# Fourteen block-product pairs instead of eleven, two rooms for their weights, and two u chunks moved behind the first v chunks

## The chip, the cores and the metric

The kernel runs on one core of a Trainium2 chip. The metric is the device time of one execution in microseconds, the median of several runs. Engines are named as the profile names them: PE (TensorE), DVE (VectorE), ACT (ScalarE), POOL (GpSimd), SP (SyncE, here only a queue of DMA issues).

## The reference, cut to what matters

One encoder layer on 256 tokens of width 1024: a modulated norm, a joint projection, two kinds of attention, an output projection, a second modulated norm, and then PEER, a retrieval of single-neuron experts, which takes most of the time. The reference gathers experts per token:

```python
ub = jnp.take(u_tab, ib, axis=0)            # 16384 experts x 1024
a  = jnp.einsum('td,ted->te', xb, ub)
w  = gb * jax.nn.gelu(a, approximate=False)
vb = jnp.take(v_tab, ib, axis=0)
y  = jnp.einsum('te,ted->td', w, vb)
```

Each token uses 8 x 16 experts with softmax gates. After it: x + gate2 * y, and a last norm.

## The kernel before, in words

The kernel gathers nothing. The 16384 experts are 128 chunks of 128. For each chunk i it computes a = u[i] times all 256 tokens (the first expert matmul), Gelu(a) times a gate table that is zero where a token does not use an expert, and adds weights times v[i] to y (the second expert matmul).

All weights are fp32 and are split in two fp32r parts: ACT copies `raw` to `hi` (L96), DVE or POOL computes `lo = raw - hi` (L97). A product is then three matmuls (`mm3`, L138 to L141): high by high, high by low, low by high. An `order` list names every unit of weights with a kind: "b" gives its L97 to POOL, "c" to DVE, and "s" marks a part of a pair, whose L97 is DVE's and which lies in the tile already. `unit()` hands out the units in that order and prepares one ahead (LEAD is 1). In the expert stages there are three buffers for `raw`, four for `hi`, three for `lo`: the `lo` of a unit can be written only when PE has done with the unit three before it, and a load can start only when the split of the unit three before has read its `raw`. All these loads are issued on SP, in order.

Stages, in order: projections, attention, the output projection, then the routing beside the first 36 u chunks (AHEAD), whose results lie in the tile GA, 256 columns to a chunk. Then the one-hot stage: for each of 64 groups of four tokens PE builds the gate table by one-hot matmuls (`gp`, L851), and between them runs u chunks 36 to 127 (`u_chunk`, 24 matmuls of 256 columns each into one of two PSUM buffers), followed by Gelu on ACT (L867) and the product with the gates on DVE (L868) into GB. A u chunk can start only when the PSUM buffer of the chunk two before it has been read by L868. BESIDE is the count of u chunks in this stage, HOLD how many of them are kept back until after the last group; BESIDE - HOLD is 89.

Then the second expert matmul, over a `plan` of steps. A plain step is one v chunk: weights of the experts (`gated`: ACT L883, DVE L884, three `wx` buffers), one unit of v, and 12 matmuls of 512 columns into the four PSUM accumulators `yp`. The last three chunks are done together at the end, so that the closing work on the first half of the tokens can begin early.

Some neighbouring chunks i and i+1 are done as a pair: a 2x2 by 2x2 block product by Strassen's scheme in Winograd's form, in seven products instead of eight. A product has three matmuls, so a pair has 21 matmuls instead of 24. For it DVE has to form four differences of v blocks (`pair_t13`, L917; `pair_t24`, L921 and L922), split them (`pair_split`, L925 on ACT, L926 on DVE), and form and split differences of the expert weights (`pair_s`, L934, L936, L937; `pair_a`, L943, L944). The pair's v chunks are loaded to a room inside GA (`bb`, the cells of chunks 12 to 19, whose values are used up by then) and the differences to `bt` (cells 20 to 27). Two parts of the room go through `unit()` as kind "s". `todo` places the steps of a pair a number of plan steps ahead of it: the load 6, `pair_s` 5, `pair_t13` 4, `pair_t24` 3, the splits 2 and 1.

SEVEN = (31, 8, 112) makes pairs of chunks 31, 39, ... 111: eleven, with six plain steps between two. The rows of `gate2` (another 8 DVE reductions, in GA cells 0 to 11) run at steps 12 to 28. After the last pair, `fold` takes one operation per plain step: it adds the pairs' accumulators and the residual up.

The order in which each engine gets its instructions is worked out when the kernel is built, from the program order, the dependencies and a list scheduler's estimate of times; DVE, ACT and SP then execute their lists strictly in that order.

Of the kernel before, what the change touches and what calls it, by code (L numbers as in the profile page):

```python
# [11 lines left out]
AF = mybir.ActivationFunctionType  # L12
# [4 lines left out]
S = 256  # L17
HD = 64
NH = 8
NKEY = 128  # L20
# [2 lines left out]
BIG = 1e30  # L23
LOW = -3e38
AHEAD = 36
BESIDE = 92
LEAD = 1
LATE = 5
E2AT = 0
HOLD = 3  # L30

SEVEN = (31, 8, 112)
ENDLEAD = 2
LAST = 3
FG0 = (("p", 0, 512), ("p", 512, 1024))
# [35 lines left out]
def body(tc, xT, cols, ada, w_in, e2, w_out, wq, sk, u, v, fg, const, dil, out):  # L71
    nc = tc.nc
    with ExitStack() as top:
# [29 lines left out]
        order = []  # L103
# [8 lines left out]
        order += [(wq[i], "b") for i in range(16)]  # L112
        order += [(u[i], "b") for i in range(AHEAD + BESIDE)]

        seven = [i for i in range(*SEVEN[:1], SEVEN[2]) if (i - SEVEN[0]) % SEVEN[1] == 0]
        plan = [i for i in range(NKEY - LAST) if i - 1 not in seven]
        parts = []
        for i in plan:
            order += [(p, "s") for p in range(2)] if i in seven else [(v[i], "c")]
        order += [(v[i], "c") for i in range(NKEY - LAST, NKEY)]  # L120
        ready = []
        loaded = []
# [3 lines left out]
        def unit():  # L126
            while len(ready) <= min(taken[0] + lead[0], len(order) - 1):
                i, kind = len(ready), order[len(ready)][1]
                if kind == "s":
                    ready.append(split(i, parts[order[i][0]], nc.vector))  # L130
                    continue
                taken[1] += kind == "a"
                eng = nc.gpsimd if kind == "b" or kind == "a" and taken[1] % 2 else nc.vector
                ready.append(split(i, loaded.pop(0) if loaded else load(i), eng))
            taken[0] += 1
            return ready[taken[0] - 1]

        def mm3(ps, wh, wl, ah, al, first, last):  # L138
            nc.tensor.matmul(ps, wh, ah, start=first, stop=False)  # L139
            nc.tensor.matmul(ps, wh, al, start=False, stop=False)  # L140
            return nc.tensor.matmul(ps, wl, ah, start=False, stop=last)  # L141

        def mmT(ps, hl, act):
            h = hl[0].rearrange("p (k c) -> p k c", k=8)
            l = hl[1].rearrange("p (k c) -> p k c", k=8)
            for k in range(8):
                ins = mm3(ps, h[:, k, :], l[:, k, :], act[0][:, k, :], act[1][:, k, :], k == 0, k == 7)
            return ins
# [13 lines left out]
        def act_tiles(name):  # L162
            return tuple(P0.tile([128, 8, S], F32R, tag="h" + x, name=name + x) for x in "hl")
# [19 lines left out]
        with ExitStack() as pre:  # L183
# [129 lines left out]
            for i in range(2):  # L313
                ps = PP.tile([128, 512], F32, tag="acc", name="silp")
# [314 lines left out]
            for i in range(NQ):  # L629
                hl = unit()  # L630
                ps = PM.tile([128, 512], F32, tag="mm", name="ps")
# [13 lines left out]
            for k in range(8):  # L645
                b = mod[:, 3, k:k + 1]
                if k % 2 == 0:
                    tt = PP.tile([128, 512], F32, tag=("PT", "acc")[k // 2 % 2], name="h2t")
                t, hi = tt[:, k % 2 * S:(k % 2 + 1) * S], h2[0][:, k, :]
# [7 lines left out]
            GA = GAP.tile([128, AHEAD, S], F32)  # L657
# [3 lines left out]
            def u_chunk(i):  # L661
                hl = unit()
                ps = PM.tile([128, 512], F32, tag="mm", name="ps")
                mm_ins[i] = mmT(ps[:, :S], hl, h2).ins
                return ps
# [149 lines left out]
        def cell(i, t0, t1):  # L815
            return GA[:, i, t0:t1] if i < AHEAD else GB[:, i - AHEAD, t0:t1]

        done = AHEAD
# [8 lines left out]
        def one_hots(n):  # L827

            if 4 * n >= S:
                return  # L830
            t0 = 4 * n
            jm = WK.tile([128, 4, 128], F32R, tag="wx", name="jm", bufs=WXB)
            gi = WK.tile([128, 4, 2, 128], F32R, tag="gi", name="gi", bufs=2)
            nc.vector.tensor_tensor(jm, iotaG[:, None, :].to_broadcast([128, 4, 128]),  # L834
                                    jT[:, t0:t0 + 4, None].to_broadcast([128, 4, 128]), op=OP.is_equal)
            for t in range(4):
                nc.vector.scalar_tensor_tensor(gi[:, t, :, :], iotaG[:, None, :].to_broadcast([128, 2, 128]),  # L837
                                               iT[:, t0 + t:t0 + t + 1],
                                               gT.bitcast(F32)[:, :, t0 + t, None].to_broadcast([128, 2, 128]),
                                               op0=OP.is_equal, op1=OP.mult)  # L840
            hot[n] = jm, gi
# [3 lines left out]
        for n in range(S // 4):  # L845
# [17 lines left out]
            one_hots(n + 2)  # L863
            while done - AHEAD < (BESIDE if t0 + 4 == S else (n + 1) * (BESIDE - HOLD) // (S // 4)):
                te = t0 + 4
                ps = u_chunk(done)
# [8 lines left out]
        with tc.tile_pool(name="py", bufs=1, space=bass.MemoryType.PSUM) as PY:  # L875
# [11 lines left out]
            def give(i, hl, T, f):  # L887
                ts, fs = slice(T * 128, (T + 1) * 128), slice(f * 512, (f + 1) * 512)
                wh, wl = W[i]
                mm3(yp[T][f], wh[:, ts], wl[:, ts], hl[0][:, fs], hl[1][:, fs], i == 0, i == NKEY - 1)  # L890

            def row(t):
                return bass.AP(tensor=t.tensor, offset=t.offset, ap=[[0, 128], [1, D]])
# [8 lines left out]


            bl = GA[:, 12:28, :].rearrange("p (b a) t -> p b (a t)", a=2)
            bb, bt = bl[:, 0:4, :], bl[:, 4:8, :]
            parts += [bb[:, 3:4, :], bb[:, 0:3:2, :]]
            sph, spl = (t.rearrange("p (b a) t -> p b (a t)", a=2) for t in act_tiles("sp"))
            P = {}
            AS = {}

            def pair_load(i):
                for e in range(2):
                    nc.sync.dma_start(bb[:, 2 * e:2 * e + 2, :], v[i + e].rearrange("p (f c) -> p f c", f=2))

            def pair_t13(i):

                nc.vector.tensor_tensor(bt[:, 0:2, :], bb[:, 1:4:2, :], bb[:, 0:2, :], op=OP.subtract)  # L917

            def pair_t24(i):

                nc.vector.tensor_tensor(bt[:, 2, :], bb[:, 3, :], bt[:, 0, :], op=OP.subtract)  # L921
                nc.vector.tensor_tensor(bt[:, 3, :], bb[:, 2, :], bt[:, 2, :], op=OP.subtract)  # L922

            def pair_split(n, m, src):
                nc.scalar.activation(sph[:, n:m, :], src, AF.Copy)  # L925
                nc.vector.tensor_tensor(spl[:, n:m, :], src, sph.bitcast(F32)[:, n:m, :], op=OP.subtract)  # L926
# [66 lines left out]


            p1, r, c12, c21 = (bt[:, n, :] for n in range(4))
            c22 = bb[:, 0, :]
            fold = [lambda: nc.scalar.activation(p1, P[1], AF.Copy)]
            fold += [lambda o=o, x=x, y=y: nc.vector.tensor_add(o, P[x], y) for o, x, y in ((r, 6, p1), (c12, 5, r), (c21, 7, r), (c22, 7, c12))]
            for n, c in enumerate((p1, c12, c21, c22)):
                t, fs = x1[n // 2], slice(n % 2 * 512, (n % 2 + 1) * 512)  # L1000
# [5 lines left out]
            todo = {}  # L1006
            for i in seven:
                at = plan.index(i)
                for d, f in ((6, pair_load), (5, pair_s), (4, pair_t13), (3, pair_t24),
                             (2, lambda i: pair_split(0, 2, bt[:, 0:2, :])), (1, lambda i: pair_split(2, 4, bt[:, 2:4, :]))  # L1010
                             ):
                    todo.setdefault(at - d, []).append((f, i))
            for n, i in enumerate(plan):
                nxt = plan[n + 1] if n + 1 < len(plan) else NKEY - LAST
                for f, p in todo.get(n, ()):
                    f(p)
                (pair_a if nxt in seven else gated)(nxt)
                if i in seven:
                    pair_products(i)
                    if i == seven[-1]:  # L1020
                        for dst, src in ((g2b, row(g2d)), (x1[0], x1d[0]), (x1[1], x1d[1]), (fgb, row(fg))):
                            nc.sync.dma_start(dst, src)
                        fold.pop(0)()
                    continue
                hl = unit()
                for T in range(2):
                    for f in range(2):
                        give(i, hl, T, f)
                if i >= 12 and i % 2 == 0 and (i - 12) // 2 < 9:
                    gate2((i - 12) // 2)  # L1030
                if i > seven[-1] and fold:
                    fold.pop(0)()
# [115 lines left out]
```

## Time and profile before

| what | value |
|---|---|
| median of 3 runs | 979.08 us (978.34 to 982.81) |
| profiled execution, its own time | 980.62 us |
| its span, first to last instruction | 978.8 us |
| granted TensorE clock, mean of the span | 0.987 |
| PE busy | 952.0 us, 97% of the span |
| DVE busy | 783.5 us, 80% |
| ACT busy | 565.5 us, 58% |
| POOL busy | 451.2 us, 46% |
| DMA queues of the core | 193.76 MB, 198 GB/s |

Busy time is the time in which an engine had an instruction in work; matmuls overlap each other, so the pace of PE is read from the starts of successive matmuls and not from their durations. The same holds on DVE: successive instructions overlap by some 0.08 us.

### The profile page before, as it was taken

What the parts mean: (1) busy time and instruction counts of PE and PEld (TensorE: products, weight loads), DVE (VectorE), ACT (ScalarE), POOL (GpSimd) and SP (SyncE); (2) the same over time, 40 slices, a digit from 0 to 9 for tenths busy, and PEclk for the clock granted to TensorE, in tenths of its full rate; (3) what the DMA queues carried; (4) which work ended last, traced back from release to release, by engine and by line L of the source; (5) the groups of instructions that cost most, each with busy time, mean ns of one, the idle gap of its engine ahead of it and who ended that gap; (6) DMA issues with size and microseconds to landing.
All of it is one profiled execution on the core that took longest, in us unless ns stands there. A gap on an engine that the chain in (4) does not pass through costs nothing.

```text
span 978.8 us, 17367 instructions
## 1 busy us (share of the span) xinstructions
PE 952.0 (97%) x6292; PEld 867.9 (89%) x6292; DVE 783.5 (80%) x1800; ACT 565.5 (58%) x1043; POOL 451.2 (46%) x201
## 2 busy tenths in 40 slices
PE   8899998999999999999999999899999999999996
PEld 5787888999999999999999999888888888888885
DVE  6859888899992677788889887667787888887786
ACT  4366576645445666666666665454655665665653
POOL 2678457677888677777777776300000000000002
PEclk8999799999999999999999999999999999999998
DMA  9776784555554455555545555578657666656562
GB/s 349 284 262 252 260 304 160 160 173 161 184 184 141 152 165 162 170 159 165 164 161 172 155 170 156 177 268 309 222 183 261 235 200 205 195 192 209 158 206 73
DMA packets 53398, 193.76 MB, mean 198 GB/s; under 512 B 5816, under 2 KB 6080, under 8 KB 53184
## 3 DMA queue, kind: packets, MB, share of 16 engines
q1 hardware_dynamic: 52672, 191.59, 59.4%
q8 instruction: 49, 0.80, 0.3%
q10 hardware_dynamic: 576, 1.05, 0.3%
q14 instruction: 37, 0.30, 0.1%
q0 software_dynamic: 64, 0.01, 0.0%
HBM read 190.52 MB, written 2.11 MB: 197 GB/s over the span
## 4 chain that ended last, share of the span: by engine, by line
PE 83%; DVE 3%; issue 2%; ACT 1%; POOL 1%; POOLq 0%; ACTq 0%; DVEq 0%
PE ps L139 15%; PE ps L140 14%; PE ps L141 14%; PE y L140 10%; PE y L139 10%; PE y L141 10%; PE gp L851 3%; PE P L140 1%; DVE araw L217 1%; PE P L139 1%; PE P L141 1%; PE op L466 1%; PE scp L706 1%; ACT hi L96 1%; PE pTp L453 0%
## 5 line engine op out<-in xcount | busy, mean ns | idle before, releaser
L97 POOL TENSOR_TENSOR lo<-raw,hi 128x1024 fp32r<-128x1024 f32 x172 | 422.4, 2459 | 159.1 <-PE ps L141 73.5
L96 ACT ACTIVATE hi<-raw 128x1024 fp32r<-128x1024 f32 x282 | 297.2, 1057 | 187.5 <-issue 63.2
L139 PE MATMUL ps<-h2h,hi 128*128 128x256 f32 x1128 | 320.5, 285 | 3.0 <-DVE GB L868 2.6
L140 PE MATMUL ps<-h2l,hi 128*128 128x256 f32 x1128 | 319.0, 283 | 0.0
L141 PE MATMUL ps<-h2h,lo 128*128 128x256 f32 x1128 | 318.8, 283 | 0.0
L139 PEld LDWEIGHTS ps<-h2h,hi 128*128 128x128 f32 x1128 | 216.2, 192 | 4.1 <-DVE GB L868 3.0
L140 PEld LDWEIGHTS ps<-h2l,hi 128*128 128x128 f32 x1128 | 216.4, 192 | 0.0
L141 PEld LDWEIGHTS ps<-h2h,lo 128*128 128x128 f32 x1128 | 216.2, 192 | 0.0
L97 DVE TENSOR_TENSOR lo<-raw,hi 128x1024 fp32r<-128x1024 f32 x110 | 134.7, 1225 | 53.8 <-issue 44.3
L140 PE MATMUL y<-lo,wx 128*128 128x512 f32 x424 | 165.1, 389 | 0.0
L141 PE MATMUL y<-hi,wx 128*128 128x512 f32 x424 | 165.1, 389 | 0.0
L139 PE MATMUL y<-hi,wx 128*128 128x512 f32 x424 | 165.1, 389 | 0.0
L837 DVE SCALAR_TENSOR_TENSOR gi<-iotaG,iT,gT 128x256 fp32r<-128x256 f32 x256 | 113.8, 476 | 30.5 <-PE gp L851 30.5
L1063 POOL TENSOR_TENSOR GB<-GB 128x512 f32<-128x512 f32 x2 | 2.6, 1290 | 258.3 <-ACT GB L1056 258.3
L141 PEld LDWEIGHTS y<-hi,wx 128*128 128x128 f32 x424 | 79.6, 188 | 16.8
L139 PEld LDWEIGHTS y<-hi,wx 128*128 128x128 f32 x424 | 79.6, 188 | 16.7
L140 PEld LDWEIGHTS y<-lo,wx 128*128 128x128 f32 x424 | 79.6, 188 | 16.5 <-DVE lo L97 0.3
L854 DVE TENSOR_TENSOR gp<-gp,gl 128x512 f32<-128x512 f32 x64 | 44.6, 697 | 8.3 <-ACT gl L853 6.7
L883 ACT ACTIVATE wx<-GB 128x256 fp32r<-128x256 f32 x72 | 28.7, 411 | 36.5 <-PE y L141 36.1
L834 DVE TENSOR_TENSOR jm<-iotaG,jT 128x512 fp32r<-128x512 f32 x64 | 43.6, 681 | 1.6 <-ACT iotaG L823 1.6
L857 ACT ACTIVATE GB<-gp 128x368 f32<-128x368 f32 (+31 forms) x64 | 21.3, 332 | 37.4 <-DVE gp L854 37.4
L989 POOL DMA_DIRECT2D g2d<-g2r x1 | 0.6, 594 | 88.9 <-ACT wxh L943 88.9
(266 smaller groups left out, 1518.0 us busy)
## 6 DMA issues: line engine op xcount, KB each, us to landing
raw<-in_u SPq DMA_DIRECT2D x128, 512.0 KB, 3.5
raw<-in_v SPq DMA_DIRECT2D x106, 512.0 KB, 3.6
araw<-in_ada SPq DMA_DIRECT2D x20, 1024.0 KB, 5.7
raw<-in_w_in SPq DMA_DIRECT2D x24, 512.0 KB, 6.2
GA<-in_v SPq DMA_DIRECT2D x22, 512.0 KB, 4.4
raw<-in_wq SPq DMA_DIRECT2D x16, 512.0 KB, 3.6
raw<-in_w_out SPq DMA_DIRECT2D x8, 512.0 KB, 6.1
GA<-in_ada SPq DMA_DIRECT2D x8, 512.0 KB, 5.4
```

Of the source, the lines that this page charges most:

```text
L96: nc.scalar.activation(hi, raw, AF.Copy)
L97: ins = eng.tensor_tensor(lo, raw, hi.bitcast(F32), op=OP.subtract)
L139: nc.tensor.matmul(ps, wh, ah, start=first, stop=False)
L140: nc.tensor.matmul(ps, wh, al, start=False, stop=False)
L141: return nc.tensor.matmul(ps, wl, ah, start=False, stop=last)
L217: block_sum.ins = nc.vector.tensor_tensor_reduce(raw, raw, silb, 1.0, init, OP.mult, OP.add, m).ins
L834: nc.vector.tensor_tensor(jm, iotaG[:, None, :].to_broadcast([128, 4, 128]), jT[:, t0:t0 + 4, None].to_broadcast([128, 4, 128]), op=OP.is_ ...
L837: nc.vector.scalar_tensor_tensor(gi[:, t, :, :], iotaG[:, None, :].to_broadcast([128, 2, 128]), iT[:, t0 + t:t0 + t + 1], gT.bitcast(F32)[ ...
L851: nc.tensor.matmul(gp[:, t, :, :], jm[:, t, :], gi[:, t, :, :], start=True, stop=True)
L854: nc.vector.tensor_tensor(gp[:, :, 0, :], gp[:, :, 0, :], gl, op=OP.add)
L857: nc.scalar.activation(GB[:, m:, t0:t0 + 4], gv[:, done:, :], AF.Copy)
L883: nc.scalar.activation(wh, w, AF.Copy)
```

## The change

Three things. First, SEVEN becomes (31, 6, 112): pairs at 31, 37, ... 109, fourteen of them, with four plain steps between two. Second, the pairs' v chunks go by turns to two rooms, the old one and GA cells 0 to 7; `bt` stays one. `pair_s`, `pair_t13` and `pair_t24` move one plan step nearer to the pair; the load stays six steps ahead, which is now one step ahead of the previous pair. Third, BESIDE becomes 90 and HOLD 1: u chunks 126 and 127 leave the one-hot stage and are done behind v chunk 0 and v chunk 1, and the L97 of their weights goes to DVE (kind "c") instead of POOL.

```diff
-BESIDE = 92
+BESIDE = 90
...
-HOLD = 3
-
-SEVEN = (31, 8, 112)
+HOLD = 1
+
+SEVEN = (31, 6, 112)
...
-            order += [(p, "s") for p in range(2)] if i in seven else [(v[i], "c")]
+            order += [(seven.index(i) % 2 * 2 + p, "s") for p in range(2)] if i in seven else [(v[i], "c")]
+            if i < NKEY - AHEAD - BESIDE:
+                order.append((u[AHEAD + BESIDE + i], "c"))
...
-            bb, bt = bl[:, 0:4, :], bl[:, 4:8, :]
-            parts += [bb[:, 3:4, :], bb[:, 0:3:2, :]]
+            bt = bl[:, 4:8, :]
+            rooms = [bl[:, 0:4, :], GA[:, 0:8, :].rearrange("p (b a) t -> p b (a t)", a=2)]
+            for bb in rooms:
+                parts += [bb[:, 3:4, :], bb[:, 0:3:2, :]]
...
             def pair_load(i):
+                bb = rooms[seven.index(i) % 2]
...
-            c22 = bb[:, 0, :]
+            c22 = rooms[0][:, 0, :]
...
-                for d, f in ((6, pair_load), (5, pair_s), (4, pair_t13), (3, pair_t24),
+                for d, f in ((6, pair_load), (4, pair_s), (3, pair_t13), (2, pair_t24),
...
+                if done < NKEY:
+
+                    ps = u_chunk(done)
+                    nc.scalar.activation(ps[:, :S], ps[:, :S], AF.Gelu)
+                    nc.vector.tensor_mul(cell(done, 0, S), ps[:, :S], cell(done, 0, S))
+                    done += 1
```

`pair_t13` and `pair_t24` choose their room by the same line as `pair_load`.

## Rows read from the trace of the kernel before

**Rows 1.** Busy time by stretch of the span: stretch, length, then each engine.
```profile
600.00:630.00 30.00, 27.22 (x219) 26.39 (x218) 21.93 (x40) 15.92 (x34) 14.88 (x7) 1.00 0.51 153
630.00:713.00 83.00, 83.00 (x368) 68.63 (x367) 61.13 (x86) 43.48 (x65) 0.59 (x1) 1.00 0.75 256
713.10:925.30 212.20, 212.20 (x938) 175.77 (x937) 177.00 (x260) 130.48 (x192) 0.00 (x0) 1.00 0.64 208
```

**Rows 2.** Waits of PE from 600 us to the end: total us, times, longest.
```profile
PE ps L139 <- DVE GB L868: 2.6, 2, 1.9
PE ps L139 <- ACT GB L870: 0.2, 1, 0.2
```

**Rows 3.** Timeline, all engines, around the first PE wait of rows 2.
```profile
614.64 2.62 POOL L97 TENSOR_TENSOR lo<-raw,hi 128x1024 fp32r<-128x1024 f32 x1 [0.47 <-ACT wx L883]
614.91 2.63 DVE L884 TENSOR_TENSOR wx<-GA,wx 128x256 fp32r<-128x256 f32 x1
616.88 0.28 PE L140 MATMUL ps<-h2l,hi 128*128 128x256 f32 x1
617.00 0.28 PE L141 MATMUL ps<-h2h,lo 128*128 128x256 f32 x1
...
617.46 0.41 DVE L868 TENSOR_TENSOR GB<-ps,GB 128x256 f32<-128x256 f32 x1
617.51 2.39 POOL L97 TENSOR_TENSOR lo<-raw,hi 128x1024 fp32r<-128x1024 f32 x1 [0.26 <-PE ps L141]
617.79 2.25 DVE L934 TENSOR_TENSOR sr<-GA 128x128 f32<-128x128 f32 x1
...
617.93 0.39 PE L139 MATMUL ps<-h2h,hi 128*128 128x256 f32 x1 [0.65 <-DVE GB L868]
```

**Rows 4.** Timeline, all engines, around the second PE wait of rows 2.
```profile
620.78 0.28 PE L141 MATMUL ps<-h2h,lo 128*128 128x256 f32 x1
...
622.10 0.36 ACT L867 ACTIVATE ps<-ps 128x256 f32<-128x256 f32 x1
...
622.49 0.42 DVE L868 TENSOR_TENSOR GB<-ps,GB 128x256 f32<-128x256 f32 x1 [0.52 <-ACT ps L867]
622.83 1.22 DVE L97 TENSOR_TENSOR lo<-raw,hi 128x1024 fp32r<-128x1024 f32 x1
...
622.97 0.39 PE L139 MATMUL ps<-h2h,hi 128*128 128x256 f32 x1 [1.91 <-DVE GB L868]
```

**Rows 5.** Timeline of PE: first matmul of a pair, first of the step behind it.
```profile
713.32 0.39 PE L139 MATMUL P<-sph,sx 128*128 128x512 f32 x1
...
718.08 0.39 PE L139 MATMUL y<-hi,wx 128*128 128x512 f32 x1
```

**Rows 6.** DVE busy (instructions) in one period from pair to pair.
```profile
734.43:755.51 21.08, 17.71 (x26) 1.00 0.75 248
```

**Rows 7.** Timeline of DVE in that period: its idle times, and pieces of its order.
```profile
734.43 1.22 DVE L97 TENSOR_TENSOR lo<-raw,hi 128x1024 fp32r<-128x1024 f32 x1 [0.81 <-issue]
...
737.83 1.22 DVE L97 TENSOR_TENSOR lo<-raw,hi 128x1024 fp32r<-128x1024 f32 x1 [1.84 <-issue]
...
745.73 1.22 DVE L97 TENSOR_TENSOR lo<-raw,hi 128x1024 fp32r<-128x1024 f32 x1
746.86 0.42 DVE L884 TENSOR_TENSOR wx<-GB,wx 128x256 fp32r<-128x256 f32 x1
747.20 1.22 DVE L926 TENSOR_TENSOR spl<-GA,sph 128x1024 fp32r<-128x1024 f32 x1
748.70 0.42 DVE L884 TENSOR_TENSOR wx<-GB,wx 128x256 fp32r<-128x256 f32 x1 [0.28 <-ACT wx L883]
...
752.80 1.23 DVE L97 TENSOR_TENSOR lo<-GA,hi 128x1024 fp32r<-128x1024 f32 x1 [0.41 <-PE y L140]
```

**Rows 8.** DMA issues, 630 to 925 us: count, KB each, median us to landing.
```profile
raw<-in_v SPq DMA_DIRECT2D x89, 512.0 KB, 3.6
GA<-in_v SPq DMA_DIRECT2D x22, 512.0 KB, 4.4
```

More of the change, by code (lines that the diff above doesn't have):

```diff
@@ L915, in pair_t13 @@
             def pair_t13(i):
+                bb = rooms[seven.index(i) % 2]
                 nc.vector.tensor_tensor(bt[:, 0:2, :], bb[:, 1:4:2, :], bb[:, 0:2, :], op=OP.subtract)
             def pair_t24(i):
+                bb = rooms[seven.index(i) % 2]
                 nc.vector.tensor_tensor(bt[:, 2, :], bb[:, 3, :], bt[:, 0, :], op=OP.subtract)
```

## The prediction

> **What bounds the kernel now.** I read the busy time by stretch first. From the first v chunk on, PE is busy in every microsecond: 83.00 of 83.00 and 212.20 of 212.20, at full clock [rows 1]. There only fewer matmuls, or a new wait of PE, can move the end. Just ahead of it, between 600 and 630 us, 2.78 us are missing (30.00 less 27.22). The waits of PE say what they are: from 600 us on it waits three times, twice for L868, the DVE operation that empties the PSUM buffer of a u chunk [rows 2]. So the change has two places where it can gain, the count of matmuls and this border, and one where it can lose: DVE, which has the pairs' extra work and is busy 177.00 of 212.20 us [rows 1].
>
> **Fewer matmuls.** Three more pairs, each with 21 matmuls in place of 24: nine less. A pair's 21 take 718.08 - 713.32 = 4.76 us [rows 5], 0.227 us each. The period confirms it: six plain steps of 12 and a pair of 21 are 93 matmuls, times 0.227 is 21.1 us, and the period lasts 21.08 [rows 6]. Nine matmuls are **2.04 us**. As long as PE stays without waits, this is sure.
>
> **The border.** Matmuls of a u chunk follow each other at 0.12 us (616.88, 617.00) [rows 3], so a chunk takes 24 x 0.12 = 2.88 us. After 617.00 the next starts at 617.93, which loses 0.93 - 0.12 = 0.81 us [rows 3]. After 620.78 the next starts at 622.97, which loses 2.19 - 0.12 = 2.07 us [rows 4]. Together **2.88 us**. Why is L868 late? Two DVE instructions that stand ahead of it are stretched: L884 takes 2.63 us here and 0.42 us elsewhere [rows 3, 7], and L934, on half as many columns, takes 2.25. Both end as a POOL L97 ends: POOL runs from 614.64 to 617.26 and from 617.51 to 619.90 [rows 3], DVE is through at 617.54 and 620.04. So POOL's split holds up a DVE operation with two inputs in SBUF, and L868 stands behind it. ACT's Gelu is dragged along, at 622.10 for a chunk whose last matmul was issued at 617.00, since the ACT copy of `sr` stands ahead of it [rows 4].
>
> The two POOL splits in question are those of chunks 126 and 127: with three `lo` buffers the split that begins at 617.51 waited for the chunk that ended near 617.3, chunk 124. The change makes exactly these two DVE work. No POOL split is left after chunk 125's, so nothing stretches L884 and L934, and both waits should go. The Trainium skill, "SBUF — State Buffer", section "Who interferes with whom", states that a DVE instruction with two SBUF inputs contends with a GpSimd instruction that reads SBUF, and whichever issues first blocks the other fully. By that rule the sum is -2.88 us here; read without it, as a DVE that simply has too much queued, moving two more splits to DVE would give back nothing.
>
> What the border could cost instead: after the last group there were five u chunks on PE, 5 x 2.88 = 14.4 us, and now three, 8.6 us, before v chunk 0 comes. PE gets there at 617.12 (end of chunk 124) + 2.88 = 620.0. Chunk 0 needs its `wx` and its split. Its `wx` was ready in the trace of before by 617.5 in spite of the block [rows 3]. Its split, at 622.83 before [rows 4], waits now for the `lo` of chunk 123 and not of 125, that is two chunks of 2.88 us earlier, and for a load that takes the place of chunk 126's. If it came at 622.83 all the same, it would end at 624.05 and PE would wait 4.05 us, so the border lies between +1.2 (4.05 - 2.88) and -2.88. I take the lower end, since what made DVE late is gone and the buffers come free early. The moved chunks themselves cost nothing more: 48 matmuls in either place, and in between v chunk 1 covers Gelu and L868 of chunk 126 by 12 x 0.227 = 2.7 us; they need no PSUM buffer that a pair holds before step 31. Their splits and L868 are some 3 us of DVE in a stretch where DVE is busy 61.13 of 83.00 us [rows 1].
>
> **DVE with pairs closer together.** In a period of before DVE is busy 17.71 us of 21.08 [rows 6]. The period after has two plain steps less: each has one L97, 746.86 - 745.73 = 1.13 us from start to start, and one L884, 747.20 - 746.86 = 0.34 us [rows 7]. So DVE needs 17.71 - 2 x 1.47 = 14.77 us, and PE 4 x 12 + 21 = 69 matmuls x 0.227 = 15.65 us. DVE is then 94% occupied, with 0.88 us to spare per period. Whether that is enough depends on DVE's own waits. In the period of before they are 0.81 + 1.84 + 0.28 + 0.41 = 3.34 us [rows 7], all but 0.28 of it around the pair, which does not change. If they stayed, the period would be 14.77 + 3.34 = 18.11 us, 2.46 over PE's, thirteen times: +32 us. Below, the cost is nothing. I take nothing, because of what these waits are: the first two are for a `lo` buffer that PE still reads (the split after the pair's start at 734.43, the next at 737.83 when the pair's first part is done, 15 matmuls or 3.4 us into it), and so is the 0.41. They show that DVE is ahead, and they shrink by as much as it falls behind. Followed through by the same order, with pair start at 0: split of the first plain step 0.2 to 1.4 and its `wx`; wait to 3.6; second split to 4.8; L917, two `wx`, third split to 7.7; the two halves of L921 and L922, fourth split to 10.1; `wx`, both L926 to 12.7; the rest of the pair's preparation to 16.8. The next period then begins at 16.8 instead of 15.9, and its wait for 3.6 (19.2) absorbs that. The splits are needed at 4.8, 7.5, 10.2, 12.9: every one has 2.4 us or more in hand. The closest is the low part of the pair's `wx`, ready at 16.8 and read by the fourth product at about 18.1.
>
> The other engines: ACT has fewer plain copies in a period that gets shorter, and is at 130.48 of 212.20 now [rows 1]. The loads per microsecond stay: 8 chunks in 21.08 us before, 6 in 15.65 after. A pair's loads stand on SP ahead of the previous pair's step; with one room they would hold every `raw` load behind them until that pair's parts are split, with two they start at once. They land in 4.4 us, a `raw` load in 3.6 [rows 8], against three plan steps of at least 2.7 us up to L917. The second room is free: gate2's last reading of cells 0 to 7 is at step 28, the first load into it at step 30.
>
> **The sum.** Against the profiled execution's 980.62 us: -2.04 - 2.88 = -4.92, 975.70 us. That execution lies 1.54 us above the median of the runs, so for the median I say 979.08 - 4.92 = **974.2 us**.
>
> **The rivals.**
>
> *Only the matmuls count* (the border keeps its waits, as another operation on DVE or ACT holds up L868 or chunk 0): -2.04, 977.0 us. For it: five chunks of cover become three, and DVE gets two more splits there. Against it: both waits end with a POOL split that is no longer there [rows 3].
>
> *DVE costs a little*: in some periods an order that the scheduler chose leaves a pair's part late. For it: 0.88 us to spare, and ACT and DVE wait for each other in chains (0.28) [rows 7]. If half of the 3.34 us of waits stay, 1.67, the period is 0.79 us over; if that happens in a third of thirteen periods, it takes 3.4 us back, 977.6 us.
>
> *DVE becomes the bound, slower*: its waits stay above a point in every period. The point is 0.88 us for any loss, and 0.88 + 4.92/13 = 1.26 us for no gain at all; to be 0.5% slower it is 0.88 + 9.8/13 = 1.64 us. With 1.84 us, the largest of them [rows 7], staying whole: 13 x 0.96 = 12.5 us back, 986.7 us. For it: the wait stands ahead of L917, which need not wait but is queued behind. Against it: it is a wait for PE.
>
> **How the numbers follow.** Both terms whole: 0.58. Only the matmuls: 0.15. DVE costs a little: 0.17. DVE is the bound: 0.10. The range: down to 972.5, since the runs of before lie up to 0.74 us below their median and up to 3.7 above it and I can't tell the gain of one wait better than that; up to 979.5, which takes in the second and nearly all of the third case. About half a per cent, 4.9 us, is what a measurement of this kernel can tell from no change, and my forecast lies on that line, which is at 979.08 - 4.90 = 974.18. Of the first case I count 0.44 as beyond it, and another 0.01 from elsewhere: faster 0.45; same 0.45; slower 0.10, the last case.
>
> **What would show it.** The pace and the fewer matmuls: 15.65 us from pair to pair. The border: no PE wait for L868 after the last group, v chunk 0 directly behind chunk 125, L884 and L934 at their usual lengths. DVE: idle times in a period that add up to less than 0.9 us and no PE row of the second matmul that waits for DVE's L97, L926 or L944. I am wrong if PE waits at pair starts, or if chunk 0 comes before its split.

## The result, and the profile after

| | before | after |
|---|---|---|
| median of 7 runs | 980.02 us (978.34 to 982.81) | 973.89 us (971.79 to 975.04) |
| profiled execution, its own time | 980.62 us | 971.98 us |
| span, mean granted TensorE clock | 978.8 us, 0.987 | 970.2 us, 0.996 |

The ratio is 0.994 with a 95% interval from 0.9928 to 0.9952: 6.1 us faster, between 4.7 and 7.1. The forecast was 974.2.

The profiled executions lie 8.6 us apart, and more than three of these are not the change's. Instruction lists of all engines are the same up to the last group of the one-hot stage, yet the first u matmul (of the first expert matmul) starts at 179.4 us before and at 175.6 after. So I compare by stage, from the first u matmul on. The columns are differences of starts in the trace: first matmul into `ps` from h2, last one-hot matmul `gp`, first matmul of a pair `P`, end of the span.

| kernel, profiled execution | first u matmul | to last `gp` | `gp` to first pair | first pair to end |
|---|---|---|---|---|
| before | 179.4 | 428.5 | 105.4 | 265.5 |
| after | 175.6 | 428.7 | 102.7 | 263.2 |
| after, a second time (e9) | 178.3 | 428.5 | 102.5 | 263.2 |

The border gives 2.7 to 2.9 us, the pairs 2.3, together 5.1 to 5.2. What the medians show beyond that, some 1 us of 6.1, is within their interval, and the start of the kernel alone differs by 3 us between executions (last section).

The waits of PE from 590 us on, after (total us, times, longest; L870 and L872 are the L868 and L870 of before). The entry for the gate product, 2.6 us in [rows 2], is gone:

```profile
PE ps L141 <- ACT GB L872: 0.4, 1, 0.4
```

The timeline of DVE behind the last group, after; L886 is L884 of before, L941 is L934:

```profile
610.15 0.52 DVE L864 TENSOR_TENSOR GB<-gp,GB 128x348 f32<-128x348 f32 x1
610.59 0.36 DVE L941 TENSOR_TENSOR sr<-GA 128x128 f32<-128x128 f32 x1
610.88 0.41 DVE L886 TENSOR_TENSOR wx<-GA,wx 128x256 fp32r<-128x256 f32 x1
611.21 1.21 DVE L97 TENSOR_TENSOR lo<-raw,hi 128x1024 fp32r<-128x1024 f32 x1
612.35 0.41 DVE L870 TENSOR_TENSOR GB<-ps,GB 128x256 f32<-128x256 f32 x1
612.68 0.74 DVE L886 TENSOR_TENSOR wx<-GA,wx 128x256 fp32r<-128x256 f32 x2
613.35 0.28 DVE L941 TENSOR_TENSOR sr<-GA 128x128 f32<-128x128 f32 x1
```

The split of v chunk 0 (611.21) is done four microseconds before PE comes to it at 616.64, and no L886 or L941 there is longer than 0.43 us, against 2.63 and 2.25 in [rows 3]. POOL's last split of the stage begins at 608.40, and PE goes over without a gap:

```profile
608.40 2.40 POOL L97 TENSOR_TENSOR lo<-raw,hi 128x1024 fp32r<-128x1024 f32 x1 [2.14 <-PE ps L143]
```

```profile
616.40 0.28 PE L142 MATMUL ps<-h2l,hi 128*128 128x256 f32 x1
616.52 0.28 PE L143 MATMUL ps<-h2h,lo 128*128 128x256 f32 x1
616.64 0.40 PE L141 MATMUL y<-hi,wx 128*128 128x512 f32 x1
```

A period from pair to pair, after, by the busy times (stretch, length, PE, PEld, DVE, ACT, POOL, clock), which answers to [rows 6]: 15.64 us, PE busy in all of it.

```profile
738.32:753.96 15.64, 15.64 (x71) 12.95 (x70) 14.54 (x23) 10.20 (x15) 0.00 (x0) 1.00 0.75 268
```

DVE in that period, from the timeline, answers to [rows 7]. It has one idle time left, 1.06 us, before the pair's first L933 (L926 before):

```profile
738.32 1.22 DVE L97 TENSOR_TENSOR lo<-raw,hi 128x1024 fp32r<-128x1024 f32 x1
739.47 0.42 DVE L886 TENSOR_TENSOR wx<-GB,wx 128x256 fp32r<-128x256 f32 x1
740.95 1.23 DVE L933 TENSOR_TENSOR spl<-GA,sph 128x1024 fp32r<-128x1024 f32 x1 [1.06 <-ACT sph L932]
742.09 1.22 DVE L97 TENSOR_TENSOR lo<-raw,hi 128x1024 fp32r<-128x1024 f32 x1
...
753.96 1.23 DVE L97 TENSOR_TENSOR lo<-raw,hi 128x1024 fp32r<-128x1024 f32 x1
```

So DVE needs 15.64 - 1.06 = 14.58 us per period. Of the four idle times of [rows 7] all three for a `lo` buffer are gone: DVE no longer runs into the end of its `lo` buffers. What is left is a wait for ACT's copy of the pair's differences, 12.4 us in twelve times from 720 to 900 us.

### The profile page after: what moved, and what is told of

It is laid out like the page before. It is cut to its first block, busy times and chain, and to the rows that moved or that the text cites. A ratio compares the mean times of both kernels' runs of the same rounds, so it can differ in the third digit from the quotient of the medians.

```text
span 970.2 us, 17414 instructions
## 1 busy us (share of the span) xinstructions
PE 942.9 (97%) x6283; PEld 860.3 (89%) x6283; DVE 798.1 (82%) x1832; ACT 571.7 (59%) x1052; POOL 446.7 (46%) x199
## 3 DMA queue, kind: packets, MB, share of 16 engines
HBM read 190.52 MB, written 2.11 MB: 199 GB/s over the span
## 4 chain that ended last, share of the span: by engine, by line
PE 83%; DVE 3%; issue 2%; POOL 1%; ACT 1%; DMA 0%; POOLq 0%; ACTq 0%; DVEq 0%
PE ps L141 15%; PE ps L142 14%; PE ps L143 14%; PE y L141 10%; PE y L142 10%; PE y L143 10%; PE gp L853 3%; PE P L141 1%; PE P L142 1%; PE P L143 1%; DVE araw L219 1%; PE scp L708 1%; PE op L468 1%; POOL lo L97 1%; PE pTp L455 0%
## 5 line engine op out<-in xcount | busy, mean ns | idle before, releaser
L97 POOL TENSOR_TENSOR lo<-raw,hi 128x1024 fp32r<-128x1024 f32 x170 | 418.0, 2462 | 156.0 <-PE ps L143 73.7
L96 ACT ACTIVATE hi<-raw 128x1024 fp32r<-128x1024 f32 x276 | 290.7, 1056 | 172.1 <-issue 61.6
L141 PE MATMUL y<-hi,wx 128*128 128x512 f32 x400 | 155.8, 389 | 0.0
L142 PE MATMUL y<-lo,wx 128*128 128x512 f32 x400 | 155.7, 389 | 0.0
L143 PE MATMUL y<-hi,wx 128*128 128x512 f32 x400 | 155.6, 389 | 0.0
L97 DVE TENSOR_TENSOR lo<-raw,hi 128x1024 fp32r<-128x1024 f32 x106 | 128.9, 1225 | 32.5 <-issue 20.8
L143 PEld LDWEIGHTS y<-hi,wx 128*128 128x128 f32 x400 | 75.1, 188 | 15.8
L142 PEld LDWEIGHTS y<-lo,wx 128*128 128x128 f32 x400 | 75.1, 188 | 15.6 <-DVE lo L97 0.2
L141 PEld LDWEIGHTS y<-hi,wx 128*128 128x128 f32 x400 | 75.1, 188 | 15.5
L885 ACT ACTIVATE wx<-GB 128x256 fp32r<-128x256 f32 x66 | 25.9, 411 | 47.5 <-PE y L143 47.5
L933 DVE TENSOR_TENSOR spl<-GA,sph 128x1024 fp32r<-128x1024 f32 x28 | 34.2, 1222 | 12.4 <-ACT sph L932 12.4
L859 ACT ACTIVATE GB<-gp 128x368 f32<-128x368 f32 (+31 forms) x64 | 21.3, 333 | 37.7 <-DVE gp L856 37.7
```

The source lines that it names most:

```text
L96: nc.scalar.activation(hi, raw, AF.Copy)
L97: ins = eng.tensor_tensor(lo, raw, hi.bitcast(F32), op=OP.subtract)
L859: nc.scalar.activation(GB[:, m:, t0:t0 + 4], gv[:, done:, :], AF.Copy)
L885: nc.scalar.activation(wh, w, AF.Copy)
```

## The experiments

Ratios are to the kernel before on the same chip, with their 95% interval. Stages are those of the table above.

**e1 and e2: each half alone.**

```diff
 # e1, against after
-BESIDE = 90
-HOLD = 1
+BESIDE = 92
+HOLD = 3
 # e2, against before: BESIDE = 90, HOLD = 1, u[126] and u[127] into `order`
 # behind v[0] and v[1] as "c", and u_chunk behind their steps
```

e1: 

> Fourteen pairs and two rooms, but the one-hot stage as before (BESIDE 92, HOLD 3). If the two gains are separate, this has the nine matmuls alone: 2.04 us less than before, 978.0 against 980.0, and the two PE waits for the u chunks' gate product at the border stay (2.6 us). From pair to pair 15.64 us. If the pairs only paid because the border had been cleared, or DVE gives some of it back, the gain is smaller than 1 us and PE waits in the second expert matmul.

e2: 

> The two u chunks moved behind v chunks 0 and 1, their splits on DVE; eleven pairs and one room as before. If the border is a gain of its own: 2.9 us less than before, 977.1 against 980.0, no PE wait for the u chunks' gate product, 21.08 us from pair to pair. If the border needs nothing but was hidden, less than 1 us.

Measured: e1 976.31 us, ratio 0.9972 (0.9958 to 0.9986); e2 976.37 us, 0.9968 (0.9954 to 0.9981). By stage, e1 has 263.2 us from the first pair to the end, as after, and keeps 2.6 us of PE waits for L870 at the border; e2 has 102.5 from `gp` to the first pair, 3.0 less than before, and 265.2 to the end. Each half is a gain of its own, and they add up. In e1 the border took 107.0 us in the profiled execution, 1.6 more than before with the same waits; the last section shows why.

**e3: the kernel before, the two splits on DVE, nothing moved.**

```diff
-        order += [(u[i], "b") for i in range(AHEAD + BESIDE)]
+        order += [(u[i], "b" if i < NKEY - 2 else "c") for i in range(AHEAD + BESIDE)]
```

> The kernel before with one edit: the splits of u chunks 126 and 127 go to DVE, the chunks stay where they were. If POOL's split is what holds DVE up: the stretched operations (2.6 and 2.3 us) are back at 0.4 and 0.3, both PE waits go or shrink below 0.5 us together, 977 to 977.5. If the order of DVE's and ACT's work behind the last group is the cause, DVE has 2.3 us more to do there and the waits stay or grow: 980 to 982.

Measured: 974.5 us, ratio 0.9956 (0.9937 to 0.9974). The border takes 102.4 us, within 0.1 of e2, and PE has no wait for L868 from 590 us on. The median is 2.5 us below what was expected; by stage only the 3.0 us of the border are there, and the start of the kernel (last section) can hide or add as much. The DVE operations that were stretched are short, in the timeline of e3:

```profile
612.47 0.75 DVE L884 TENSOR_TENSOR wx<-GA,wx 128x256 fp32r<-128x256 f32 x2
613.14 0.28 DVE L934 TENSOR_TENSOR sr<-GA 128x128 f32<-128x128 f32 x1
613.34 0.28 DVE L934 TENSOR_TENSOR sr<-sr,GA 128x128 f32<-128x128 f32 x1
613.66 0.29 DVE L934 TENSOR_TENSOR sr<-GA,sr 128x128 f32<-128x128 f32 x1
```

DVE has more to do there than before and is through earlier. It was POOL's split, not the amount of work.

**e4: the changed kernel, the two moved splits on POOL.**

```diff
-                order.append((u[AHEAD + BESIDE + i], "c"))
+                order.append((u[AHEAD + BESIDE + i], "b"))
```

> The changed kernel with one edit: the splits of the two moved chunks stay on POOL. If POOL's split holds up DVE operations with two inputs in SBUF, some DVE operation of the first v steps is again stretched to 1.5 to 2.6 us; PE waits for it only if it stands ahead of a u chunk's gate product or of a split that is due, which I put at 0 to 2 us over the changed kernel, so 974 to 976. If the place of the chunks is what counts, no DVE operation is stretched and the time is the changed kernel's within 0.5 us.

Measured: 974.41 us, ratio 0.995 (0.9931 to 0.9969); from `gp` to the first pair 104.6 us, 1.9 to 2.1 over the changed kernel. The size was as expected, the way was not. No DVE operation was stretched to 1.5 us at the border; the longest single L886 there has 0.64. PE goes through the border without a wait and loses its time some 80 us after the last `gp`, which is at 607.3 here. The timeline of POOL, DVE and PE in e4:

```profile
617.06 2.42 POOL L97 TENSOR_TENSOR lo<-raw,hi 128x1024 fp32r<-128x1024 f32 x1 [3.35 <-DVE sr L941]
...
622.37 2.40 POOL L97 TENSOR_TENSOR lo<-raw,hi 128x1024 fp32r<-128x1024 f32 x1 [2.89 <-PE y L142]
624.41 0.64 DVE L886 TENSOR_TENSOR wx<-GA,wx 128x256 fp32r<-128x256 f32 x1 [2.80 <-ACT wx L885]
...
687.40 1.28 DVE L990 CUSTOM_DVE_ANT_0 GA<-GA,col 128x1024 f32<-128x1024 f32 x1 [3.90 <-DMA GA<-in_ada]
688.61 1.22 DVE L97 TENSOR_TENSOR lo<-raw,hi 128x1024 fp32r<-128x1024 f32 x1
689.88 0.49 PE L142 MATMUL y<-lo,wx 128*128 128x512 f32 x1 [1.41 <-DVE lo L97]
```

DVE waits 3.90 us for a load of `in_ada`, and the split that PE wants stands behind it. In the changed kernel (last `gp` at 604.3) the same L990 waits 1.18 us:

```profile
682.47 1.28 DVE L990 CUSTOM_DVE_ANT_0 GA<-GA,col 128x1024 f32<-128x1024 f32 x1 [1.18 <-DMA GA<-in_ada]
683.68 1.22 DVE L97 TENSOR_TENSOR lo<-raw,hi 128x1024 fp32r<-128x1024 f32 x1
```

That is 78.2 us after the last `gp` there and 80.1 in e4, so the loads run some 2 us later against PE, in a stretch where the DMA engines are busy 0.88 of 665 to 685 us. The trace shows where the lag begins. POOL's splits take 2.4 us where DVE's take 1.2 and give their `raw` buffers back later: the loads of v chunks 2 and 4, which go into the buffers of u chunks 126 and 127, are issued 12.2 and 17.5 us after the last `gp`, right behind the two POOL splits, against 11.1 and 16.3 in the changed kernel. The `in_ada` load that L990 waits for lands at 80.0 us after it, against 78.1 in the profile after and 76.9 in e9. That the one lag is the other, carried through all the loads between, is likely but not shown: there is one profile of e4.

What e4 does show is that a split on POOL does not slow DVE by itself, only where DVE has certain operations in its span. Those are held until the split ends. When L884 started in [rows 3], 2.35 us of POOL's split were left, and it took 2.63; L934 met 2.11 us and took 2.25; the L886 of e4, at 624.41, met 0.36 and took 0.64. An operation with one input in PSUM is not held: L868 at 612.86 in the kernel before, within the POOL split of 611.76 to 614.17, takes its usual 0.42 us. The Trainium skill, "SBUF — State Buffer", section "Who interferes with whom", says that a DVE operation with two inputs in SBUF and a GpSimd instruction that reads SBUF contend. [Rows 3], e3 and e4 agree with it. In e4 DVE had little of that kind to do while POOL ran: it sat idle 1.61 of the 2.42 us of the first split and most of the second.

**e5 and e6: more work for DVE.** The first difference of each pair is computed twice (e5) or three times (e6), with the same result.

```diff
-                nc.vector.tensor_tensor(bt[:, 0:2, :], bb[:, 1:4:2, :], bb[:, 0:2, :], op=OP.subtract)
+                for _ in range(2):    # e6: 3
+                    nc.vector.tensor_tensor(bt[:, 0:2, :], bb[:, 1:4:2, :], bb[:, 0:2, :], op=OP.subtract)
```

e5: 

> The changed kernel with DVE's 128x1024 difference of each pair done twice: 1.13 us more DVE work in each period, nothing else. DVE needs 14.58 us of a period's 15.64 by the trace of the changed kernel. If this sum is the limit: 15.71 us, 0.07 over PE's, thirteen times, 0.9 us in all, so within 1.5 us of the changed kernel's 974. If the waits of DVE in a period are real losses, they add to it: some 1 us per period, 987 us.

e6: 

> The same three times: 2.27 us more. If the sum is the limit: 14.58 + 2.27 = 16.85 us from pair to pair, 1.21 over PE's, thirteen times 15.7 us: 990 us. If PE has more in hand than the sum says: less than 980 us. If the waits add to it: above 1000 us.

Measured: e5 973.81 us, 0.9955 (0.9937 to 0.9973); e6 981.76 us, 1.003 (1.0012 to 1.0048). From the first pair to the end: e5 263.2 us, nothing lost; e6 272.0, 8.8 more than after, where the sum gave 15.7. (Another 1.1 us or so are lost in e6 before the first pair: its border takes 103.8 us.) In e6 DVE is busy 179.37 of the 180 us from 720 to 900, so it is the bound there, and PE waits for DVE, and once for ACT:

```profile
PE y L142 <- DVE lo L97: 4.0, 6, 0.8
PE y L143 <- DVE wx L886: 0.6, 1, 0.6
PE y L141 <- ACT wx L885: 0.6, 1, 0.6
```

Both sums were too high. In e5 a full period of DVE lasts 15.57 us and not 15.71 (from one pair's first split of its differences to the next pair's), which is still below PE's 15.64: e5 does not make DVE the bound, so it says nothing of what happens beyond. In e6 nine full periods of DVE, from 765.86 to 916.25, last 16.71 us on average and not 16.85 (16.6 in most, up to 17.0). From the fourth product of the first pair to that of the last, 710.35 to 922.49, PE has thirteen periods of 16.32 us on average, and the third to the fifth of them still have PE's own 15.64 to 15.68. So of the missing 6.9 us about 1.8 are the sum's error, 13 x 0.14, and the rest, 13 x (16.71 - 16.32) = 5.1, is what DVE had done ahead: a DVE that is slower than PE first uses up its lead, and only then does PE wait. For e6 this split of the difference is an estimate; e12 shows the lead more plainly.

**e7, e10 and e12: more pairs.** SEVEN is (31, 5, 112), seventeen pairs, in e7 and again in e10 beside the changed kernel (e9); in e12 it is (31, 4, 112), twenty-one, with the load five steps ahead.

```diff
-SEVEN = (31, 6, 112)
+SEVEN = (31, 5, 112)    # e12: (31, 4, 112)
```

e7: 

> Pairs every five chunks: seventeen, three plain steps between two. PE needs 57 matmuls, 12.92 us, per period, DVE 14.58 - 1.47 = 13.11. If the sums decide, DVE is the bound by 0.19 us, sixteen times 3.0 us, against nine matmuls less, 2.0 us: 1 us above the changed kernel, 975 us, and PE waits for DVE. If waits add to DVE's sum the time is above 980; if PE were still the bound, 972.

e9: 

> The changed kernel once more, on the same chip as the next three, to compare them with it: 5 to 6 us less than before.

e10: 

> Seventeen pairs once more, on one chip with the changed kernel. If its nine further matmuls are all gain: 2.0 us less than the changed kernel. If the first result was chance: the same within 1 us.

e12: 

> Pairs every four chunks: twenty-one, two plain steps between two (the load five steps ahead). PE needs 45 matmuls, 10.2 us per period, DVE 12.97 - 1.47 = 11.50 by the period of seventeen pairs. DVE is the bound: 1.3 us, twenty times 26 us, of which some 7 us may come out of the work DVE has done ahead, against 2.7 us of matmuls less: about 16 us above seventeen pairs, 985 to 992 us, slower than before. If what DVE does ahead absorbs most of it, below 978 us.

Measured: e7 972.49 us, 0.9929 (0.9907 to 0.9951); e9 973.2, 0.994 (0.9926 to 0.9955); e10 970.79, 0.9924 (0.9908 to 0.9941); e12 989.99, 1.0109 (1.0089 to 1.013). Seventeen pairs have 261.1 us from the first pair to the end in both profiles, 2.0 less than fourteen: nine matmuls, all gain. The expectation of e7, PE waiting for DVE and 975 us, missed: DVE's period came out at 12.97 us and not 13.11. There DVE is full. Two periods of e7, DVE busy:

```profile
769.88:782.85 12.97, 12.94 (x22) 1.00 0.63 202
782.85:795.82 12.97, 12.94 (x22) 1.00 0.60 202
```

DVE's 12.97 us are 0.05 over PE's 12.92, sixteen times 0.8 us, and PE still has no wait for it from 590 us on: it is paid from the lead. With twenty-one pairs the bound has changed sides, 279.7 us from the first pair to the end. The waits of PE and the busy times of e12 (PE, PEld, DVE, ACT, POOL, clock):

```profile
PE P L141 <- ACT sph L932: 15.4, 14, 1.1
```

```profile
800.00:900.00 100.00, 90.11 (x387) 71.57 (x386) 98.74 (x155) 65.59 (x96) 0.00 (x0) 1.00 0.52 184
```

PE waits at the pairs for ACT's copy L932, which itself follows DVE's differences; DVE is the one that is full. Here the lead can be seen: from fourth product to fourth product the first three periods last 10.20, 10.20 and 10.21 us, PE's own pace, and from the seventh on 11.6. Twenty periods of 11.6 would cost 28 us over PE's 10.2; the stage is 18.6 us longer than with seventeen pairs, which is 21.3 with the twelve matmuls that it has less. The lead paid the other 7, as expected.

**e8: one room for all pairs.**

```diff
-            rooms = [bl[:, 0:4, :], GA[:, 0:8, :].rearrange("p (b a) t -> p b (a t)", a=2)]
+            rooms = [bl[:, 0:4, :]] * 2
-                for d, f in ((6, pair_load), (4, pair_s), ...
+                for d, f in ((4, pair_load), (4, pair_s), ...
```

> Fourteen pairs, but both turns use the old room, and the load stands four steps ahead instead of six (one step behind the previous pair). In the trace of the changed kernel the previous pair's parts are split 1.1 us before that pair begins, and the difference that needs the new load comes 10.3 us after its begin, against a landing of 4.4 us: so no cost, within 1 us of the changed kernel. If the load that waits on SP for its room holds the loads behind it, as I wrote in the prediction, ACT waits for loads and PE for splits: 2 us or more above it.

Measured: 971.53 us, 0.9934 (0.9914 to 0.9955); 263.2 us from the first pair to the end, as with two rooms, and ACT waits for `raw` loads 0.5 us in all from 720 to 914 us (0.8 in the profile after). The second room brings nothing, with the load two steps later; one room with the load still six steps ahead was not run. Why it brings nothing shows in the profile after. The load of the next pair goes to the other room there, and yet SP issues it only when DVE has split the last part of the pair before:

```profile
735.74 1.22 DVE L97 TENSOR_TENSOR lo<-GA,hi 128x1024 fp32r<-128x1024 f32 x1
...
736.98 0.81 SPq L918 DMA_DIRECT2D GA<-in_v  x2
```

The split ends at 736.96, and SP has waited 4.9 us for it. In e8 the same two times are 736.31 and 736.33. Why the load waits for a room that is not its own no run shows.

**e11: fourteen pairs, nothing moved, the two splits on DVE** (e1 with the edit of e3).

> Fourteen pairs and two rooms, u chunks 126 and 127 in their old place (BESIDE 92, HOLD 3), their splits on DVE. If only the engine of the two splits counts at the border, this is the changed kernel within 1 us, no PE wait for the gate product. If the place counts too, 1 to 3 us above it.

Measured: 974.4 us, 0.9952 (0.9936 to 0.9968); stages 102.4 and 263.2, those of the changed kernel. The place of the two u chunks counts for nothing.

## Why the prediction was right

*Fewer matmuls, 2.04 us.* Right: 2.3 in both profiles of the changed kernel against the one of before, 2.0 between e2 and e8 (265.2 against 263.2), and once more 2.0 from fourteen to seventeen pairs.

*The border, 2.88 us.* Right in size (2.7 and 2.9; 3.0 in e2 and e3) and in cause: POOL's split of u chunks 126 and 127, as e3 shows by that edit alone. The bound of +1.2, a late v chunk 0, came near nothing. To move the chunks as well was not needed, as e3 and e11 show.

*DVE with pairs closer together, no cost.* Right, and for the reason given: the waits for `lo` buffers shrank to none. The sum of 14.77 us was 0.2 too high against 14.58. So the idle time left, 1.06 us, is above the 0.9 that the prediction named as its sign, and the point from which DVE was to cost, 0.88 us per period, is 1.06: e5 stays below it, with 15.57 - 14.58 = 0.99, and loses nothing. Beyond that point the sum treats a period as if it stood alone; e6, e7 and e12 show that the lead pays first. The rival "DVE costs a little" is excluded by the thirteen periods after, every one of 15.64 us in both profiles with no wait of PE for DVE. The one in which DVE is the bound needs pairs every four chunks (e12), not every six.

*With one room the pair's load holds the `raw` loads on SP, with two it starts at once.* Wrong, though the time does not hang on it. With two rooms the load also starts only when the parts of the pair before are split (736.98 behind 736.96); that is before this pair begins (738.29), and the `raw` loads behind it still come in time. e8 loses nothing.

*The sum.* -4.92 us against -5.1 to -5.2 by stage. That the median itself, 973.89, lies within 0.3 us of the forecast is partly luck: the forecast started from 979.08, the median of three runs, and seven gave 980.02, while the gain of the medians was 6.1 and not 4.92. "Only the matmuls" is excluded by e2 and e3.

## What to carry to other kernels

A wait of the bounding engine is first to be asked which instruction ahead in the releasing engine's list is longer than its like, and what else runs in just that span; here one engine assignment for two splits was worth more than three further pairs. An engine that is less than full on average can be filled nearly to the top while it works ahead of the bound, and a small deficit is paid from that lead before it is paid in time. So seventeen pairs, with DVE's sum 0.05 us a period over PE's, still gained (970.79 us against 973.2 on the same chip, 2.0 by stage); twenty-one, 1.4 us over, cost 17 us against fourteen.

## What the runs showed of the hardware that was not expected

*A gap of PE can be followed by a lower clock.* In e1 the two waits at the border are those of before to a tenth, but then the granted clock falls (busy times of e1: PE, PEld, DVE, ACT, POOL, clock):

```profile
614.00:619.00 5.00, 4.36 (x36) 4.15 (x36) 5.00 (x4) 1.07 (x2) 4.74 (x2) 1.00 0.63 171
619.00:625.00 6.00, 4.08 (x29) 3.88 (x29) 3.36 (x7) 3.09 (x5) 0.14 (x1) 0.88 0.48 136
625.00:632.00 7.00, 7.00 (x43) 6.59 (x43) 3.22 (x4) 2.67 (x4) 0.00 (x0) 0.86 0.41 139
```

The timeline of PE in e1 shows where: matmuls of 256 columns follow at 0.12 us, and from 623.66 to 626.9 at 0.21, which is the lower level, 1.2 GHz.

```profile
620.01 0.28 PE L143 MATMUL ps<-h2h,lo 128*128 128x256 f32 x1
622.21 0.39 PE L141 MATMUL ps<-h2h,hi 128*128 128x256 f32 x1 [1.92 <-DVE GB L870]
...
623.50 0.36 PE L142 MATMUL ps<-h2l,hi 128*128 128x256 f32 x1
623.66 0.42 PE L143 MATMUL ps<-h2h,lo 128*128 128x256 f32 x1
623.87 0.41 PE L141 MATMUL ps<-h2h,hi 128*128 128x256 f32 x1
```

Sixteen matmuls that start 0.09 us later each make 1.5 of the 1.6 us by which the border of e1 is longer than before's, where the clock stayed at 1.00 through the same gaps. That the gaps brought the clock down is a reading of this one profile, and how often it happens was not measured. The profiles without the gaps show 1.00 from 600 to 632 us.

*The start of the kernel has two lengths.* In the fourteen profiles the first u matmul comes at 175.3 to 175.8 us (seven) or at 178.3 to 179.4 (seven), whatever the kernel, and the granted clock between 100 and 120 us is 0.91 or 1.00 in the first seven and 0.74 in the others. The profile of before is a long one, that of after a short one, and that of e9, the same kernel as after, a long one. Before, then after:

```profile
100.00:120.00 20.00, 17.88 (x107) 16.27 (x107) 15.55 (x43) 11.99 (x33) 9.30 (x4) 0.74 0.82 303
```

```profile
100.00:120.00 20.00, 18.41 (x139) 16.56 (x139) 19.18 (x54) 14.19 (x39) 9.80 (x5) 0.91 0.81 306
```

Nineteen matmuls of 256 columns that start 0.21 us apart from 109.3 to 113.2 us before start 0.12 apart in the profile of after. These 3 us are as much as each half of the change gives, which is why single times of this kernel say little and the stages were compared.
